# A two-layer decoder trunk on one core: moving operands read from two alternating places, and merged products in the down projections

## The chip, the core and the metric

The kernel runs on one NeuronCore of a Trainium2 chip. The metric is device time in microseconds of one execution, from the first to the last instruction with what lies around them. Three runs of the kernel before gave 567.93, 568.34 and 568.43 us.

## What is computed

One sequence of 256 tokens with 1024 features passes two layers. Layer 0 mixes tokens with a gated recurrence (RG-LRU), layer 1 with native sparse attention in three branches. Each mixer is followed by a squared-ReLU MLP with 4096 hidden features. Everything is float32. Cut to what matters:

```python
def _sq_relu_mlp(h, w_up, w_down):
    u = jax.nn.relu(h @ w_up)
    return (u * u) @ w_down

def reference(x, ...):
    for i in range(2):
        h = _rmsnorm(x, norm_mix[i])
        x = x + (_rglru_mixer(h, ...) if i == 0 else _nsa_mixer(h, ...))
        h = _rmsnorm(x, norm_ffn[i])
        x = x + _sq_relu_mlp(h, mlp_w_up[i], mlp_w_down[i])
    return _rmsnorm(x, norm_final)
```

Nearly all the arithmetic is in matrix products: the input and output projections of both mixers and, above all, the four products of the two MLPs.

## The kernel before

**Layout.** Activations lie transposed: features on the 128 partitions, the 256 tokens in the free dimension. A product takes a 128 x 128 block of weights as the stationary operand and 256 tokens of activations as the moving one, and adds into a PSUM bank of 512 columns, of which the first 256 are used (`zcols`, line 328).

**The split product.** The fast matmul type (`F32R`) keeps fewer bits than float32. So each weight piece and each activation is split in a high part, rounded to that type, and a low part, the rest. `mm3` (line 317) makes three matmuls of each 128 x 128 block: high weights with high activations, high weights with low ones, low weights with high ones. The piece of low with low is left out. The gates of the recurrence (line 686) and some small products of the attention use full float32 instead.

**Stages.** Layer 0: eight convolution chunks, gates, scan, eight branch chunks (`conv`, `gate`, `scan`, `branch`, `product`, lines 644 to 731), then the output projection. `mlp` (line 766): 32 up chunks of 8 blocks each, whose result is squared and split by `up_post` (line 776) into the tile `uhl`, high half in columns 0 to 255, low half in 256 to 511; then eight down chunks of 32 blocks each, added to the residual stream `xt` by `residual` (line 521). Layer 1: projections, compression, value projection (`values`, line 998, where the weights are the moving operand and are 304 or 256 columns wide), scores, softmax, output projection, then `mlp` again. In the last down chunk of layer 1 the residual is put into PSUM by the matmuls themselves (`seeded`, line 799).

**Weights.** 172 pieces arrive by DMA from one queue in a fixed order. ScalarE or VectorE rounds a piece to its high part (`split_hi`, line 271), VectorE subtracts for the low one (`split_lo`, line 281). In the MLPs `tick` does one such step per piece, up to six pieces ahead.

**The order.** In the MLPs the program's text sets the order of each engine. In the two mixers a planner (`Plan`, line 80) orders tasks by costs and due times that are written beside them; it sees a task's keys and cost, not its access patterns. Each engine then runs its instructions in that order.

**What the change touches.** The operands of `mm3` in `proj` (line 389), `conv`, `out` (line 758), `mlp` and `out_t` (line 1194); the moving weights of `values`; and the instructions that write those operands or read the products: lines 662, 723, 730, 731, 778, 784, 785, 887, 899, 936, 1190 and 1192. Two of them, as they stand before:

```python
dve.scalar_tensor_tensor(t, z, 0.0, rs, op0=OP.max, op1=OP.mult)      # 778
act.activation(uh[m], t, AF.Square)                                   # 784
```

Of the kernel before, what the change touches and what calls it, by code (L numbers as in the profile page):

```python
# [19 lines left out]
P = 128  # L20
# [199 lines left out]
def trunk_kernel(ctx: ExitStack, tc: tile.TileContext, x_in, vec_in, const_in, w2_in, wts, out):  # L220
# [71 lines left out]
    def later(fn):  # L292
        deferred.append(fn)
# [39 lines left out]
    class Section:  # L333
# [141 lines left out]
    hh, hl = hhl[:, :, 0], hhl[:, :, 1]  # L475
    acc = spool.tile([P, S], F32, name="acc")
# [48 lines left out]
    with ExitStack() as ph:  # L525
# [101 lines left out]
        xb, r_t, i_t, y_t, t_t, xbh, xbl = ([x[:, m] for m in range(8)] for x in (xb_b, r_b, i_b, y_b, t_b, xbh_b, xbl_b))  # L627
# [16 lines left out]
        def conv(m, t):  # L644
            b = nextbank()
            if m < NFINE:
                wh, wl, _ = sec.weight("in", 8 + m, t)
                z, zk = sec.bank(("in", 8 + m), b, zcols), ("ps", b)
                for k in range(KC):
                    def run(e, k=k):  # L650
                        w = slice(k * P, (k + 1) * P)
                        mm3(z(), wh[:, w], wl[:, w], hh[:, k], hl[:, k], k == 0, k == KC - 1)
# [9 lines left out]
            add("dve", 0.34, lambda e: e.tensor_tensor(x[:, 3:], z(), rs, op=OP.mult), r=[zk, "rs"], w=[xk], t=t)  # L662
# [58 lines left out]
        def branch(m, t):  # L721
            z, zk = sec.proj("in", m, nextbank(), t, PJ)
            add("dve", 0.34, lambda e: e.tensor_tensor(y_t[m], z(), rs, op=OP.mult), r=[zk, "rs"], w=[("y", m)], t=t + 2.6)

        def product(m, t):
            yk, hk, lk = keys("y", m), keys("xbh", m), keys("xbl", m)
            y, h, l_, x = (pair(z, m) for z in (y_b, xbh_b, xbl_b, t_b))
            add("act", 0.53, lambda e: e.activation(y, y, AF.Gelu_apprx_tanh), r=["tab"], w=yk, t=t)
            add("dve", 0.6, lambda e: e.tensor_tensor(y, y, x, op=OP.mult), r=keys("t", m), w=yk, t=t)
            add(HI2, copy(h, y), r=yk, w=hk, t=t)  # L730
            add("dve", 0.6, diff(l_, y, h), r=yk + hk, w=lk, t=t)
# [34 lines left out]
    def mlp(layer, epilogue, first, last=None):  # L766
        with ExitStack() as ph:
# [29 lines left out]
            for m in range(8):  # L797
                z = next(zrot)[:, :S]
# [612 lines left out]
```

## Time and profile before

| what | value |
|---|---|
| median of three runs (lowest, highest) | 568.34 us (567.93, 568.43) |
| span of the profiled execution | 566.4 us, so 1.9 us of the median lie around it |
| mean granted TensorE clock | 0.997 |
| TensorE busy | 559.3 us, 99% |
| VectorE busy | 407.6 us, 72% |
| ScalarE busy | 343.9 us, 61% |
| moved by DMA | 103.66 MB, 183 GB/s |

The profiled execution's whole time is not listed apart from its span, so sums are made against the span of 566.4 us and the 1.9 us are added. Busy time of TensorE counts matmuls whose ends are modelled; its pace is read from the distance between starts. A mean over the span hides that stages differ, so the rows below are taken by stretch where that matters.

### The profile page before, as it was taken

To read this page: it belongs to the slowest core of one execution; us is meant where nothing else is said; L and a number is where in the kernel's file an instruction comes from. 1 tells how busy PE (TensorE), PEld (TensorE's weight loads), DVE (VectorE), ACT (ScalarE), POOL (GpSimd) and SP (SyncE) were. 2 spreads that over 40 slices of the span, in tenths; PEclk is the share of its full clock that TensorE was granted. 3 is DMA by queue.
4 is the path that set the end of the run, shared out by engine and by line. 5 is a ranking of instruction groups with operands and counts; after the bars stand their busy time and mean duration, and the time that the engine had idled before them with its cause. 6 is when DMAs were issued, how large, how long until landed. Compare 5 with 4: busy or idle time off the path is not lost.

```text
span 566.4 us, 12406 instructions
## 1 busy us (share of the span) xinstructions
PE 559.3 (99%) x4902; PEld 552.9 (98%) x4902; DVE 407.6 (72%) x873; ACT 343.9 (61%) x670; POOL 40.1 (7%) x55
## 2 busy tenths in 40 slices
PE   9999999999999999999999999999999999999995
PEld 9989999999999999999999999999999999999995
DVE  6899989776676565466839999999767775563532
ACT  7699675866564443354647999875855664443421
POOL 1000000000000121131000000000000000222310
PEclk9999999999999999999999999999999999999998
DMA  8936467566667456555765431264766667566402
GB/s 319 407 91 220 117 219 247 176 204 192 188 192 249 155 189 217 190 181 175 276 188 166 140 99 57 75 224 138 221 200 192 196 200 233 154 202 221 132 1 74
DMA packets 33225, 103.66 MB, mean 183 GB/s; under 512 B 3856, under 2 KB 8080, under 8 KB 33168
## 3 DMA queue, kind: packets, MB, share of 16 engines
q1 hardware_dynamic: 32624, 102.42, 56.1%
q8 instruction: 38, 0.62, 0.5%
q10 hardware_dynamic: 544, 0.46, 0.2%
q14 instruction: 19, 0.16, 0.1%
HBM read 99.23 MB, written 1.05 MB: 177 GB/s over the span
## 4 chain that ended last, share of the span: by engine, by line
PE 99%; DVE 0%; ACT 0%; DVEq 0%; POOL 0%; issue 0%; POOLq 0%
PE bank L318 28%; PE bank L319 28%; PE bank L320 28%; PE bank L1177 3%; PE bank L686 2%; PE bank L1159 2%; PE bank L1105 1%; PE bank L1106 1%; PE bank L567 1%; PE bank L1012 1%; PE bank L1013 1%; PE bank L1014 1%; PE bank L953 1%; DVE xg L1295 0%; PE bank L1287 0%; DVEq L1406 0%
## 5 line engine op out<-in xcount | busy, mean ns | idle before, releaser
L318 PE MATMUL bank<-hhl,whi 128*128 128x256 f32 x768 | 213.1, 278 | 0.0
L319 PE MATMUL bank<-hhl,whi 128*128 128x256 f32 x768 | 212.4, 277 | 0.0
L320 PE MATMUL bank<-hhl,wlo 128*128 128x256 f32 x768 | 212.3, 276 | 0.0
L318 PEld LDWEIGHTS bank<-hhl,whi 128*128 128x128 f32 x768 | 144.5, 188 | 0.1
L287 DVE TENSOR_TENSOR wlo<-raw,whi 128x1024 fp32r<-128x1024 f32 x115 | 143.2, 1266 | 1.9 <-ACT whi L278 1.9
L319 PEld LDWEIGHTS bank<-hhl,whi 128*128 128x128 f32 x768 | 144.5, 188 | 0.1
L320 PEld LDWEIGHTS bank<-hhl,wlo 128*128 128x128 f32 x768 | 144.4, 188 | 0.0
L319 PE MATMUL bank<-uhl,whi 128*128 128x256 f32 x512 | 141.4, 276 | 0.0
L320 PE MATMUL bank<-uhl,wlo 128*128 128x256 f32 x512 | 141.3, 276 | 0.0
L318 PE MATMUL bank<-uhl,whi 128*128 128x256 f32 x512 | 141.3, 276 | 0.0
L278 ACT CAST whi<-raw 128x1024 fp32r<-128x1024 f32 x116 | 118.1, 1039 | 23.1 <-issue 18.8
L318 PEld LDWEIGHTS bank<-uhl,whi 128*128 128x128 f32 x512 | 96.1, 188 | 0.0
L320 PEld LDWEIGHTS bank<-uhl,wlo 128*128 128x128 f32 x512 | 96.1, 188 | 0.0
L319 PEld LDWEIGHTS bank<-uhl,whi 128*128 128x128 f32 x512 | 96.1, 188 | 0.0
L323 DVE TENSOR_TENSOR wlo<-raw,whi 128x1024 fp32r<-128x1024 f32 (+2 forms) x72 | 77.1, 1089 | 2.9 <-ACT whi L326 2.8
L326 ACT CAST whi<-raw 128x1024 fp32r<-128x1024 f32 (+2 forms) x64 | 61.2, 969 | 16.8 <-PE bank L319 7.8
L522 DVE TENSOR_TENSOR xt<-xt,bank 128x256 f32<-128x256 f32 x39 | 15.9, 417 | 74.8 <-PE bank L320 74.5
L783 ACT ACTIVATE u<-t 128x256 f32<-128x256 f32 x64 | 26.7, 418 | 58.6 <-DVE t L778 57.2
L778 DVE SCALAR_TENSOR_TENSOR t<-bank,rstd 128x256 f32<-128x256 f32 x64 | 26.9, 423 | 41.0 <-PE bank L320 40.7
L1119 ACT ACTIVATE pt<-pt,mx 128x128 f32<-128x128 f32 (+1 forms) x64 | 28.6, 450 | 1.8 <-DVE mx L1116 1.4
L785 DVE TENSOR_TENSOR uhl<-u,uhl 128x256 fp32r<-128x256 f32 x64 | 26.6, 416 | 3.0 <-ACT uhl L784 3.0
L498 ACT ACTIVATE hhl<-xt,vec 128x256 fp32r<-128x256 f32 x8 | 4.1, 510 | 39.4 <-DVE xt L522 39.4
(202 smaller groups left out, 732.6 us busy)
## 6 DMA issues: line engine op xcount, KB each, us to landing
raw<-in_dram SPq DMA_DIRECT2D x171, 512.0 KB, 4.4
raw<-in_dram SPq DMA_DIRECT2D x4, 560.0 KB, 4.6
gw<-in_dram SPq DMA_DIRECT2D x4, 512.0 KB, 8.9
raw<-in_dram SPq DMA_DIRECT2D x6, 256.0 KB, 4.9
y<-in_dram SPq DMA_DIRECT2D x2, 512.0 KB, 7.4
pT<-in_dram SPq DMA_DIRECT2D x2, 512.0 KB, 5.4
xt<-in_dram SPq DMA_DIRECT2D x3, 256.0 KB, 4.9
kl<-tl SPq DMA_DIRECT2D x8, 64.0 KB, 4.0
```

Of the source, the lines that this page charges most:

```text
L278: (act.copy if eng is None else eng.tensor_copy)(hi_t[i % NSPL][:, :n], raw_of(i)[:, :n])
L287: (eng or dve).tensor_tensor(lo[:, :n], raw_of(i)[:, :n], hi[:, :n].bitcast(F32), op=OP.subtract)
L318: pe.matmul(ps, wh, xh, start=start, stop=False)
L319: pe.matmul(ps, wh, xl, start=False, stop=False)
L320: pe.matmul(ps, wl, xh, start=False, stop=stop)
L323: return lambda e: e.tensor_tensor(o, a, h.bitcast(F32), op=OP.subtract)
L326: return lambda e: (e.copy if e is act else e.tensor_copy)(o, a)
L778: dve.scalar_tensor_tensor(t, z, 0.0, rs, op0=OP.max, op1=OP.mult)
L783: act.activation(u, t, AF.Square)
L785: later(lambda: dve.tensor_tensor(ul[m], u, uh[m].bitcast(F32), op=OP.subtract))
L1119: add("act", (0.39, 0.49)[qc], lambda e, row=row, j=j: e.activation(row, row, AF.Exp, bias=mx[:, j:j + 1], scale=-1.0, accum_out=sm[:, j:j ...
L1177: two = lambda c, w, y, **k: [e.matmul(o()[own_(hf), c0 + c.start:c0 + c.stop], w(hf), y(hf), **k) for hf in range(2)]
```

## The change

Each moving operand of the split product, formerly read in a row, is read as element 0, 128, 1, 129, ... of 256: two places, in turn. `walk` gives that view. Results land in PSUM in a row (`pairs` only gives the same 256 columns the shape 128 x 2). For tiles that hold their tokens in a row, such as `hhl`, the product's columns are then in the alternating order, and the instruction that reads them from PSUM writes its output through `walk`, which puts the tokens in order again. Tiles that are made for a product alone, `uhl`, `xbh`, `xbl`, `oh` and `ol`, are written through `walk` instead, so that the alternating reading gives tokens in order. The moving weights of `values` are put in the matching order on the host.

In the down projections `mm2` takes the place of `mm3` but in the last chunk of layer 1. One matmul with 512 moving columns takes the high weights with high and low activations side by side, into both halves of the PSUM bank; a second with 256 columns adds the low weights' product to the second half. Both halves are then added to `xt`, by two instructions.

```diff
+    def pairs(x):
+        return x.rearrange("p (a i) -> p a i", i=2)
+
+    def walk(x):
+        return x.rearrange("p (i a) -> p a i", i=2)
+
+    def walks(x):
+        return x.rearrange("p k (i a) -> p k a i", i=2)
+
     def mm3(ps, wh, wl, xh, xl, start, stop):
+        ps = pairs(ps)
         pe.matmul(ps, wh, xh, start=start, stop=False)
         pe.matmul(ps, wh, xl, start=False, stop=False)
         pe.matmul(ps, wl, xh, start=False, stop=stop)
+
+    def mm2(ps, wh, wl, xhl, xh, start, stop):
+        pe.matmul(ps.rearrange("p (h a i) -> p h a i", h=2, i=2), wh, xhl.rearrange("p (h i a) -> p h a i", h=2, i=2),
+                  start=start, stop=False)
+        pe.matmul(pairs(ps[:, S:]), wl, xh, start=False, stop=stop)
...
-            xs, xk = xs or [(hh[:, k], hl[:, k]) for k in range(KC)], xk or hkey
+            xs, xk = xs or [(hhw[:, k], hlw[:, k]) for k in range(KC)], xk or hkey
...
+    hhw, hlw = walks(hh), walks(hl)
...
-            add("dve", 0.34, lambda e: e.tensor_tensor(y_t[m], z(), rs, op=OP.mult), r=[zk, "rs"], w=[("y", m)], t=t + 2.6)
+            add("dve", 0.34, lambda e: e.tensor_tensor(walk(y_t[m]), pairs(z()), walk(rs), op=OP.mult), r=[zk, "rs"], w=[("y", m)], t=t + 2.6)
...
-            uh, ul = [x[:, :S] for x in uhl], [x[:, S:] for x in uhl]
+            uh, ul = [walk(x[:, :S]) for x in uhl], [walk(x[:, S:]) for x in uhl]
...
-                dve.scalar_tensor_tensor(t, z, 0.0, rs, op0=OP.max, op1=OP.mult)
+                dve.scalar_tensor_tensor(walk(t), pairs(z), 0.0, walk(rs), op0=OP.max, op1=OP.mult)
...
-                act.activation(uh[m], t, AF.Square)
-                later(lambda: dve.tensor_tensor(ul[m], u, uh[m].bitcast(F32), op=OP.subtract))
+                act.activation(uh[m], pairs(t), AF.Square)
+                later(lambda: dve.tensor_tensor(ul[m], pairs(u), uh[m].bitcast(F32), op=OP.subtract))
...
-                        mm3(z, wh[:, w], wl[:, w], hh[:, k], hl[:, k], k == 0, k == KC - 1)
+                        mm3(z, wh[:, w], wl[:, w], hhw[:, k], hlw[:, k], k == 0, k == KC - 1)
...
-                z = next(zrot)[:, :S]
+                zf = next(zrot)
+                z, zb = zf[:, :S], zf[:, S:]
...
-                        mm3(z, wh[:, w], wl[:, w], uh[i], ul[i], i == 0 and not seeded, i == NF - 1)
+                        if seeded:
+                            mm3(z, wh[:, w], wl[:, w], uh[i], ul[i], False, i == NF - 1)
+                        else:
+                            mm2(zf, wh[:, w], wl[:, w], uhl[i], uh[i], i == 0, i == NF - 1)
...
                         residual(z, m)
+                        residual(zb, m)
...
-                                e.matmul(ps, hh[:, k, ts_], wh[:, ws], start=(k == 0), stop=False)
+                                e.matmul(ps, hh[:, k, ts_], walk(wh[:, ws]), start=(k == 0), stop=False)
...
-    wv = np.concatenate([kv(3), win[:, D + 6 * S:], kv(5)], axis=1).reshape(KC, P, NVCOL)
+    halved = lambda w: w.reshape(D, -1, 2).transpose(0, 2, 1).reshape(D, -1)
+    wv = np.concatenate([kv(3), win[:, D + 6 * S:]], axis=1), kv(5)
+    wv = np.concatenate([halved(w) for w in wv], axis=1).reshape(KC, P, NVCOL)
```

The lines left out do the same to the other operands and results named above. The planner's costs and due times are unchanged.

The order of the instructions stays what it was, but for the merge. TensorE at the end of the last down chunk of layer 0, before (uhl the activations, whi and wlo the high and low weights):

```order
L318 MATMUL bank_3107<-uhl,whi_86 128x256
L319 MATMUL bank_3107<-uhl,whi_86 128x256
L320 MATMUL bank_3107<-uhl,wlo_93 128x256
L318 MATMUL bank_3107<-uhl,whi_86 128x256
L319 MATMUL bank_3107<-uhl,whi_86 128x256
L320 MATMUL bank_3107<-uhl,wlo_93 128x256
L318 MATMUL bank_3269<-hhl,whi_87 128x256
L319 MATMUL bank_3269<-hhl,whi_87 128x256
L320 MATMUL bank_3269<-hhl,wlo_94 128x256
```

And in the changed kernel, where L333 and L335 are the two matmuls of `mm2`:

```order
L333 MATMUL bank_2890<-uhl,whi_86 128x512
L335 MATMUL bank_2890<-uhl,wlo_93 128x256
L333 MATMUL bank_2890<-uhl,whi_86 128x512
L335 MATMUL bank_2890<-uhl,wlo_93 128x256
L333 MATMUL bank_2890<-uhl,whi_86 128x512
L335 MATMUL bank_2890<-uhl,wlo_93 128x256
L328 MATMUL bank_3021<-hhl,whi_87 128x256
L329 MATMUL bank_3021<-hhl,whi_87 128x256
L330 MATMUL bank_3021<-hhl,wlo_94 128x256
```

Two matmuls of 256 columns with the high weights have become one of 512, and TensorE has 4054 rows of this kind where it had 4534, 480 fewer.

VectorE at the same place, from the last weight split ahead of the residual on, before:

```order
L287 TENSOR_TENSOR wlo_90<-raw_82,whi_83 128x1024
L522 TENSOR_TENSOR xt<-xt,bank_3107 128x256
L501 SCALAR_TENSOR_TENSOR hhl<-xt,vec,hhl 128x256
L487 TENSOR_TENSOR sq_112<-xt 128x256
L287 TENSOR_TENSOR wlo_91<-raw_78,whi_84 128x1024
L1214 TENSOR_TENSOR acc<-acc,sq_112 128x256
```

And in the changed kernel, where the residual is line 538:

```order
L287 TENSOR_TENSOR wlo_90<-raw_82,whi_83 128x1024
L538 TENSOR_TENSOR xt<-xt,bank_2890 128x256 x2
L517 SCALAR_TENSOR_TENSOR hhl<-xt,vec,hhl 128x256
L503 TENSOR_TENSOR sq_112<-xt 128x256
L287 TENSOR_TENSOR wlo_91<-raw_78,whi_84 128x1024
L1239 TENSOR_TENSOR acc<-acc,sq_112 128x256
```

The residual is there twice, ahead of the low half of the next input; all else on VectorE stands where it stood.

## Rows read from the trace of the kernel before

**Rows 1.** The page's first lines and its first part: the span, and of each engine the busy time, its share of the span and its instructions.
```profile
span 566.4 us, 12406 instructions
...
PE 559.3 (99%) x4902; PEld 552.9 (98%) x4902; DVE 407.6 (72%) x873; ACT 343.9 (61%) x670; POOL 40.1 (7%) x55
```

**Rows 2.** The view of waits, of TensorE alone: the waiting line, whom it waited for; us in total, times, the longest.
```profile
PE bank L567 <- POOL warm L562: 1.3, 1, 1.3
PE bank L1281 <- ACT sqh L1278: 0.3, 1, 0.3
```

**Rows 3.** The chain of work that ended last: its shares of the span by line, and pieces of it in order of time (start us, us, what, how many instructions of one kind in a row). L686 is the gates' product, L953 the compression's hidden layer, L1159 the transposes of the attention weights.
```profile
by line: PE bank L318 28.3%; PE bank L319 28.3%; PE bank L320 28.3%; PE bank L1177 2.6%; PE bank L686 2.4%; PE bank L1159 1.9%; PE bank L1105 1.1%; PE bank L1106 1.1%; PE bank L567 0.9%; PE bank L1012 0.8%; PE bank L1013 0.7%; PE bank L1014
...
29.64 12.95 PE bank L686 x60
...
284.14 3.62 PE bank L953 x64
...
312.87 0.65 PE bank L1159 x6
```

**Rows 4.** Groups of instructions by line and shape, of TensorE (PE) and of its weight loads (PEld): line, engine, operation, out<-in, tile, shape, count, then busy us and mean ns of one, then idle time before them. Lines 319 and 320 have the same counts as line 318.
```profile
L318 PE MATMUL bank<-hhl,whi 128*128 128x256 f32 x768 | 213.1, 278 | 0.0
...
L318 PEld LDWEIGHTS bank<-hhl,whi 128*128 128x128 f32 x768 | 144.5, 188 | 0.1
...
L318 PE MATMUL bank<-uhl,whi 128*128 128x256 f32 x512 | 141.3, 276 | 0.0
...
L318 PE MATMUL bank<-oh,whi 128*128 128x256 f32 x64 | 18.1, 283 | 0.0
...
L318 PE MATMUL bank<-xbh,whi 128*128 128x256 f32 x64 | 17.7, 276 | 0.0
...
L686 PE MATMUL bank<-xb,gw 128*128 128x256 f32 x64 | 14.1, 379 | 0.0
L1159 PE MATMUL bank<-cst,pt 128*128 128x128 f32 x96 | 13.3, 274 | 0.0
...
L1159 PEld LDWEIGHTS bank<-cst,pt 128*128 128x128 f32 x96 | 10.7, 141 | 0.5 <-issue 0.5
...
L953 PEld LDWEIGHTS bank<-pt,pT 128*64 128x64 f32 x64 | 3.5, 152 | 0.1
```

**Rows 5.** TensorE in order of time, in the down projection of layer 0: start us, us, engine, line, operation. The ends of matmuls are modelled; the pace is read from the starts. 20 rows of the same kind are left out.
```profile
199.73 0.28 PE L319 MATMUL bank<-uhl,whi 128*128 128x256 f32 x1
199.84 0.28 PE L320 MATMUL bank<-uhl,wlo 128*128 128x256 f32 x1
199.96 0.28 PE L318 MATMUL bank<-uhl,whi 128*128 128x256 f32 x1
200.07 0.28 PE L319 MATMUL bank<-uhl,whi 128*128 128x256 f32 x1
...
202.45 0.28 PE L319 MATMUL bank<-uhl,whi 128*128 128x256 f32 x1
```

**Rows 6.** Busy time by stretch: the stretch, its us, then busy us and instructions of PE, PEld, DVE, ACT and POOL, the granted clock, the DMA share and GB/s. In order: start and first convolutions; gates and scan; down projection of layer 0; attention.
```profile
0.00:20.00 20.00, 18.73 (x144) 18.73 (x144) 14.88 (x34) 14.51 (x31) 1.70 (x12) 1.00 0.92 343
20.00:60.00 40.00, 40.00 (x296) 38.35 (x297) 38.92 (x80) 38.00 (x70) 2.17 (x7) 1.00 0.56 196
...
180.00:268.00 88.00, 88.00 (x779) 88.00 (x778) 48.75 (x51) 35.63 (x41) 17.80 (x19) 1.00 0.58 193
...
300.00:380.00 80.00, 80.00 (x753) 76.41 (x752) 76.85 (x365) 69.98 (x214) 0.19 (x2) 1.00 0.39 122
```

**Rows 7.** TensorE in order of time, in the value projection of the attention (columns as in rows 5): three matmuls of 304 columns, then three of 256.
```profile
291.51 0.30 PE L1012 MATMUL bank<-whi,hhl 128*128 128x304 f32 x1
291.65 0.30 PE L1013 MATMUL bank<-wlo,hhl 128*128 128x304 f32 x1
291.79 0.30 PE L1014 MATMUL bank<-whi,hhl 128*128 128x304 f32 x1
291.93 0.28 PE L1012 MATMUL bank<-whi,hhl 128*128 128x256 f32 x1
292.04 0.28 PE L1013 MATMUL bank<-wlo,hhl 128*128 128x256 f32 x1
...
292.28 0.30 PE L1012 MATMUL bank<-whi,hhl 128*128 128x304 f32 x1
```

**Rows 8.** Groups of VectorE's instructions by line and shape (columns as in rows 4): the split of weights, the first and the last step behind an up projection, the residual.
```profile
L287 DVE TENSOR_TENSOR wlo<-raw,whi 128x1024 fp32r<-128x1024 f32 x115 | 143.2, 1266 | 1.9 <-ACT whi L278 1.9
...
L778 DVE SCALAR_TENSOR_TENSOR t<-bank,rstd 128x256 f32<-128x256 f32 x64 | 26.9, 423 | 41.0 <-PE bank L320 40.7
L785 DVE TENSOR_TENSOR uhl<-u,uhl 128x256 fp32r<-128x256 f32 x64 | 26.6, 416 | 3.0 <-ACT uhl L784 3.0
L522 DVE TENSOR_TENSOR xt<-xt,bank 128x256 f32<-128x256 f32 x39 | 15.9, 417 | 74.8 <-PE bank L320 74.5
```

**Rows 9.** TensorE in order of time at the end of layer 0 (columns as in rows 5): the last matmul of the down projection and the first of the next section.
```profile
261.38 0.28 PE L320 MATMUL bank<-uhl,wlo 128*128 128x256 f32 x1
261.50 0.28 PE L318 MATMUL bank<-hhl,whi 128*128 128x256 f32 x1
```

**Rows 10.** VectorE in order of time at the same place (in brackets the idle time before and what ended it): the last residual, and the low half of the normalised chunk 7.
```profile
261.70 0.42 DVE L522 TENSOR_TENSOR xt<-xt,bank 128x256 f32<-128x256 f32 x1 [4.61 <-PE bank L320]
262.69 0.48 DVE L501 SCALAR_TENSOR_TENSOR hhl<-xt,vec,hhl 128x256 fp32r<-128x256 f32 x1 [0.58 <-ACT hhl L498]
```

More of the change, by code (lines that the diff above doesn't have):

```diff
@@ L626, in trunk_kernel @@
         xbh_b, xbl_b = (rg.tile([P, 8, S], F32R, name=n) for n in ("xbh", "xbl"))
-        xb, r_t, i_t, y_t, t_t, xbh, xbl = ([x[:, m] for m in range(8)] for x in (xb_b, r_b, i_b, y_b, t_b, xbh_b, xbl_b))
+        xbhw, xblw = walks(xbh_b), walks(xbl_b)
+        xb, r_t, i_t, y_t, t_t, xbh, xbl = ([x[:, m] for m in range(8)] for x in (xb_b, r_b, i_b, y_b, t_b, xbhw, xblw))
         pair = lambda x, m: x[:, m // 2 * 2:m // 2 * 2 + 2]
@@ L651, in run @@
                         w = slice(k * P, (k + 1) * P)
-                        mm3(z(), wh[:, w], wl[:, w], hh[:, k], hl[:, k], k == 0, k == KC - 1)
+                        mm3(z(), wh[:, w], wl[:, w], hhw[:, k], hlw[:, k], k == 0, k == KC - 1)
                         if m == 0 and k == 1:
@@ L661, in conv @@
             bk = ("xb", m)
-            add("dve", 0.34, lambda e: e.tensor_tensor(x[:, 3:], z(), rs, op=OP.mult), r=[zk, "rs"], w=[xk], t=t)
+            add("dve", 0.34, lambda e: e.tensor_tensor(walk(x[:, 3:]), pairs(z()), walk(rs), op=OP.mult), r=[zk, "rs"], w=[xk], t=t)
             add("act", 0.49, lambda e: e.activation(xb[m], x[:, 3:], AF.Identity, bias=col(V_CB, m), scale=cw(3, m)),
@@ L722, in branch @@
             z, zk = sec.proj("in", m, nextbank(), t, PJ)
-            add("dve", 0.34, lambda e: e.tensor_tensor(y_t[m], z(), rs, op=OP.mult), r=[zk, "rs"], w=[("y", m)], t=t + 2.6)
+            add("dve", 0.34, lambda e: e.tensor_tensor(walk(y_t[m]), pairs(z()), walk(rs), op=OP.mult), r=[zk, "rs"], w=[("y", m)], t=t + 2.6)
         def product(m, t):
             yk, hk, lk = keys("y", m), keys("xbh", m), keys("xbl", m)
-            y, h, l_, x = (pair(z, m) for z in (y_b, xbh_b, xbl_b, t_b))
+            y, h, l_, x = (pair(z, m) for z in (y_b, xbhw, xblw, t_b))
+            yw = y.rearrange("p k (a i) -> p k a i", i=2)
             add("act", 0.53, lambda e: e.activation(y, y, AF.Gelu_apprx_tanh), r=["tab"], w=yk, t=t)
             add("dve", 0.6, lambda e: e.tensor_tensor(y, y, x, op=OP.mult), r=keys("t", m), w=yk, t=t)
-            add(HI2, copy(h, y), r=yk, w=hk, t=t)
-            add("dve", 0.6, diff(l_, y, h), r=yk + hk, w=lk, t=t)
+            add(HI2, copy(h, yw), r=yk, w=hk, t=t)
+            add("dve", 0.6, diff(l_, yw, h), r=yk + hk, w=lk, t=t)
         at_ = {}
@@ L854, in trunk_kernel @@
         oht, olt = (at.tile([P, 8 * S], F32R, name=n) for n in ("oh", "ol"))
-        oh, ol = ([x[:, i * S:(i + 1) * S] for i in range(8)] for x in (oht, olt))
+        ohw, olw = (walks(x.rearrange("p (k s) -> p k s", s=S)) for x in (oht, olt))
+        oh, ol = ([x[:, i] for i in range(8)] for x in (ohw, olw))
         NPT_ = 16
@@ L886, in qchunk @@
             ak, bk = ("sa", c % NQ), ("sb", c % NQ)
-            add("dve", 0.4, lambda e: e.scalar_tensor_tensor(x, z(), cst[:, C_QS + c:C_QS + c + 1], rs,
+            add("dve", 0.4, lambda e: e.scalar_tensor_tensor(walk(x), pairs(z()), cst[:, C_QS + c:C_QS + c + 1], walk(rs),
                                                              op0=OP.mult, op1=OP.mult), r=[zk, "rs"], w=[xk], t=t)
@@ L898, in kchunk @@
             x, xk, l_, lk = turn()
-            add("dve", 0.34, lambda e: e.tensor_tensor(x, z(), rs, op=OP.mult), r=[zk, "rs"], w=[xk], t=t)
+            add("dve", 0.34, lambda e, x=x: e.tensor_tensor(walk(x), pairs(z()), walk(rs), op=OP.mult), r=[zk, "rs"], w=[xk], t=t)
             x, l_ = two_blocks(x), two_blocks(l_)
@@ L935, in cproj @@
             x, xk, _, _ = turn()
-            add("dve", 0.34, lambda e: e.tensor_tensor(x, z(), rs, op=OP.mult), r=[zk, "rs"], w=[xk], t=t)
+            add("dve", 0.34, lambda e, x=x: e.tensor_tensor(walk(x), pairs(z()), walk(rs), op=OP.mult), r=[zk, "rs"], w=[xk], t=t)
             for hf in range(2):
@@ L1010, in run @@
                                 ws = slice(kk * NVCOL + c0, kk * NVCOL + c0 + ncol[b])
-                                ps = vz[h][b]()
-                                e.matmul(ps, hh[:, k, ts_], wh[:, ws], start=(k == 0), stop=False)
-                                e.matmul(ps, hh[:, k, ts_], wl[:, ws], start=False, stop=False)
-                                e.matmul(ps, hl[:, k, ts_], wh[:, ws], start=False, stop=(k == KC - 1))
+                                ps = pairs(vz[h][b]())
+                                e.matmul(ps, hh[:, k, ts_], walk(wh[:, ws]), start=(k == 0), stop=False)
+                                e.matmul(ps, hh[:, k, ts_], walk(wl[:, ws]), start=False, stop=False)
+                                e.matmul(ps, hl[:, k, ts_], walk(wh[:, ws]), start=False, stop=(k == KC - 1))
                         add("pe", 0.77, run, r=wk + [hkey[k]], w=[("ps", banks[h][0]), ("ps", banks[h][1])],
@@ L1171, in pv @@
             o = zview(("o", js[0]), 7, lambda x: x[:, :n * S])
-            cols = slice(js[0] * S, (js[-1] + 1) * S)
+            oj = slice(js[0], js[-1] + 1)
+            ow = lambda: o().rearrange("p (k a i) -> p k a i", k=n, i=2)
             def run(e):
@@ L1189, in pv @@
             ok, lk = ([(x, j) for j in js] for x in ("oh", "ol"))
-            add([("act", 0.1 + 0.24 * n, 0.0), ("dve", 0.07 + 0.27 * n, 0.2)], lambda e: copy(oht[:, cols], o())(e), r=bk, w=ok,
+            add([("act", 0.1 + 0.24 * n, 0.0), ("dve", 0.07 + 0.27 * n, 0.2)], lambda e: copy(ohw[:, oj], ow())(e), r=bk, w=ok,
                 t=t + 1.9 * n)
-            add("dve", 0.07 + 0.27 * n, lambda e: diff(olt[:, cols], o(), oht[:, cols])(e), r=bk + ok, w=lk, t=t + 1.9 * n + 0.3)
+            add("dve", 0.07 + 0.27 * n, lambda e: diff(olw[:, oj], ow(), ohw[:, oj])(e), r=bk + ok, w=lk, t=t + 1.9 * n + 0.3)
         def out_t(half, m, b, t, step):
```

## The prediction, made before the changed kernel ran

> **What bounds the kernel now.** I read the page's first part, then TensorE's waits, then its rows in order of time, because a share of 99% alone does not say what sets the pace. The span is 566.4 us and TensorE is busy for 559.3 us of it [rows 1]. It waits for others only 1.6 us in all [rows 2]. So the time is nearly the sum of the steps from one matmul start to the next, and the question is what one step costs.
>
> Of that sum the split product (lines 318 to 320) has 28.3% three times, 84.9% of 566.4 = 480.9 us [rows 3]. Its 4224 instructions are three times 768 + 512 + 64 + 64 [rows 4], so a step is 113.85 ns on average. In the down projection 24 steps take 202.45 − 199.73 = 2.72 us, or 113.3 ns each [rows 5]. The granted clock there is 1.00, the 2.4 GHz level [rows 6]; 256 columns at one per tick would be 106.7 ns. Each step thus pays a surcharge of 6.7 ns, 7.2 in the mean.
>
> Whose surcharge is it? Three kinds of row tell. The full-precision matmuls of the gates make two records each for 256 columns, and 60 records take 12.95 us: 215.8 ns, which is 512 ticks (213.3 ns) plus 2.5 [rows 3]. The transposes take 0.65 us for six, 108.3 ns [rows 3]. So where a column stays two ticks, an instruction pays about 2.5 ns, however long. In the value projection three steps of 304 columns take 0.42 us (140 ns, surcharge 13.3) and three of 256 take 0.35 us (117 ns, surcharge 10) [rows 7]. There the surcharge grows with the columns. I read it as a loss in the stream of moving columns when it runs at one per tick, and not as a fixed price of an instruction.
>
> **The change, part by part.**
>
> *Alternating reads.* Every moving operand of the split product, and that of the value projection, is read as element 0, 128, 1, 129 and so on. No row has such a stream. Bounds: at best the surcharge falls to the 2.5 ns of the gates, 106.7 + 2.5 = 109.2 ns. At worst a column costs two ticks, as in the gates, 215.8 ns. The nearest row to strided reading is the compression's hidden layer, 62 columns in steps of 16 elements: 64 records in 3.62 us, two side by side, 113 ns or 1.8 ns a column, against 0.84 in the gates [rows 3]; loads of weights may be what sets it, so it excludes nothing. I take the good end. The surcharge appears only in the full-rate stream, so feeding that stream is the narrow place, and two places could take turns to deliver, one being fetched while the other is read. That part is a guess; only the place of the loss is read from rows.
>
> The SBUF Cachelines part of the Trainium skill's page "Advanced Engine Details and Errata" (section Memory Cachelines) speaks against this: reads want at least two hits in one 16-byte line, and a new line at every access is penalised. By that rule the stream slows down, which is the third rival; no row here shows an alternating stream, so the trace neither confirms nor refutes it.
>
> *The merge.* In 15 of 16 down-projection chunks, 32 pairs each, the high weights take 512 columns at once: 480 pairs become single matmuls. At best one costs 215.8 ns [rows 3], against 2 × 109.2 = 218.4; if the surcharge stays, 2 × 113.3 = 226.7 at most. I take 215.8. It also removes 480 weight loads of 128 columns; each lies beside a matmul now [rows 4].
>
> *The sum.* Left are 4224 − 960 = 3264 steps of 256 columns and 480 of 512: 3264 × 109.2 = 356.4, 480 × 215.8 = 103.6, together 460.0 instead of 480.9: −20.9 us, of which the merge has 480 × 2.6 ns = 1.2. The value projection has 48 matmuls of each width: 48 × 140 + 48 × 117 = 12.3 us [rows 7] becomes 48 × 129.2 + 48 × 109.2 = 11.4: −0.9. Together −21.8.
>
> The isolated-gap formula of the page "TensorE: Matmul & The Clock Gate" of the Trainium skill (section Back-to-back issue gap), N/2.4 + 2.5 ns warm, gives 109.2 ns for a contiguous 256-column matmul, so by it nothing would be left to save. The trace disagrees: 113.3 ns in the loop.
>
> *What is given back.* From 20 to 60 us VectorE is busy 38.9 of 40, from 300 to 380 us 76.9 of 80 [rows 6]; a faster TensorE must wait for it there. About 230 and 312 of the steps (296 in the first window less 64 gates; nine projections of 24 and eight of 12 in the second) save 4.65 ns each: 1.1 + 1.5 us, which I count as lost. In the first 20 us the DMA share is 0.92 [rows 6]: another 120 × 4.65 = 0.6. Net −21.8 + 3.2 = −18.6.
>
> *The other engines.* 160 VectorE instructions of 256 elements and 8 of 512 now write, or read and write, alternating places, and so do 64 and 7 on ScalarE. No row has that pattern. Below, it costs nothing. Above, I double the cost per element: (1266 − 416)/768 = 1.1 ns [rows 8], so 0.28 us per instruction. In the up projections a chunk needs 1266 + 423 + 416 = 2.1 us of VectorE [rows 8] against 24 × 109.2 = 2.62 of TensorE, so up to 0.52 more is hidden. I take nothing: VectorE asks for an element every 1.1 ns, and TensorE gets one every 0.44 ns (113.3/256) from the same memory, so VectorE has more slack for a jump. The doubled price is the first rival.
>
> *The second residual.* Fifteen more instructions of 417 ns [rows 8]; VectorE has 39 us free in the down projection's 88 [rows 6]. Where the next reader is near, at the end of layer 0, the last residual starts at 261.70 and the low half of chunk 7 is done at 262.69 + 0.48 = 263.18 [rows 9, 10]. TensorE starts on the next projections at 261.50, and by its order 42 matmuls of other chunks come first: 42 × 113.3 ns = 4.8 us, so chunk 7 is wanted at 266.3. The slack of 3.1 us covers 0.42. Nothing is queued behind that residual but splits, two to five pieces ahead. In layer 1 the last chunk keeps the old form, so the end is unchanged. No DMA is added or moved.
>
> Between the profiled span and the median of the runs (568.34) lie 1.9 us, which stay. Result: 568.3 − 18.6 = 549.7 us.
>
> **The rivals.**
>
> *One: strided writes double VectorE's price.* The up projections then need 2.1 + 0.57 = 2.67 us a chunk against 2.62: 58 chunks × 0.05 = 3 us. The two tight windows pay directly: at most 16 × 0.28 = 4.5 us, and 9 × 0.28 + 4 × 0.57 = 4.8. Time 549.7 + 12.3 = 562. For it: both windows are full. Against it: VectorE is far from full elsewhere.
>
> *Two: the surcharge belongs to the weight load.* Every matmul carries its own load [rows 4], and 6.7 ns could be the hand-over. Alternation then gives nothing and only the 480 dropped loads count: 480 × 6.7 = 3.2 us, 565.1. For it: the steady step never varies, 0.11 or 0.12 us in every row of that stretch [rows 5]. Against it: the transposes carry a load each and step at 108.3, and the surcharge of 304 columns exceeds that of 256.
>
> *Three, slower: the alternating stream stalls.* Each column lies 128 elements from the one before; at two ticks a column a step costs 215.8 ns, a merged one 2 × 213.3 + 2.5 = 429.1. 3264 × 215.8 + 480 × 429.1 = 910 us instead of 481: about 998. It decides as soon as 256 alternating columns cost more than 113.9 ns. For it: the one strided row pays 1.8 ns a column. Against it: that row carries two weight loads for 62 columns.
>
> **How the numbers follow.** Forecast 0.52 (545 to 554). Rival one 0.16 (555 to 564). Rival two 0.11 (565). Rival three 0.12. Rival one without any gain on TensorE 0.03: 565 + 12 = 577, slower. No effect beyond 0.2%, which is about what a measurement of this kernel can tell: 0.06. Faster is 0.52 + 0.16 + 0.11 = 0.79, same 0.06, slower 0.12 + 0.03 = 0.15. The range of 543 to 566 holds the first three, 0.79; its lower end allows a give-back of nothing and a step down to 108.
>
> **What would show it.** Right: steps of 109 ns in the up projections, 216 and 109 alternating in the down projections, about 480 fewer TensorE instructions, and waits of TensorE on VectorE at 20 to 60 and 300 to 380 us only. Rival one: lines 778 and 785's successors well over 423 and 416 ns. Rival two: 113 ns steps in the up projections. Rival three: steps far over 114 ns there. The forecast is wrong if the step in the up projections is not within 108 to 111 ns.

## The result, and the profile after

The changed kernel takes 562.8 us in the median (562.43 to 563.95) against 568.25 for the kernel before, four runs of each: a ratio of 0.9907, 95% interval 0.9893 to 0.9921. It is faster, as forecast, but by 5.4 us and not by 18.6. The profile is that of the slowest of the four runs, 563.95 us. The page's first lines answer to [rows 1]:

```profile
span 561.8 us, 11456 instructions
...
PE 550.5 (98%) x4422; PEld 528.5 (94%) x4422; DVE 436.3 (78%) x888; ACT 358.0 (64%) x670; POOL 40.1 (7%) x55
```

The span fell by 4.6 us. TensorE is still busy for 98% of it, yet its weight loads went from 98% to 94% and VectorE from 72% to 78%. Two views say what a step costs now. First TensorE in order of time in the up projections of layer 0 (start us, us, engine, line, operation), the loop in which nothing is merged:

```profile
149.80 0.28 PE L330 MATMUL bank<-hhl,wlo 128*128 128x256 f32 x1
149.91 0.28 PE L328 MATMUL bank<-hhl,whi 128*128 128x256 f32 x1
...
151.92 0.28 PE L328 MATMUL bank<-hhl,whi 128*128 128x256 f32 x1
```

From 149.80 to 151.92 there are 19 steps, 111.6 ns each. Before it was 113.3 in the down projection [rows 5]. The same view in the down projection:

```profile
199.93 0.38 PE L333 MATMUL bank<-uhl,whi 128*128 128x512 f32 x1
200.15 0.27 PE L335 MATMUL bank<-uhl,wlo 128*128 128x256 f32 x1
200.26 0.38 PE L333 MATMUL bank<-uhl,whi 128*128 128x512 f32 x1
...
201.90 0.38 PE L333 MATMUL bank<-uhl,whi 128*128 128x512 f32 x1
```

From 199.93 to 201.90 there are six blocks, 328 ns each. Before, a block was three steps of 113.3, 340 ns. The rows' starts alternate by 0.22 and 0.11: over all 480 pairs the mean from start to start is 218.3 ns from a wide matmul to the next narrow one and 109.2 from a narrow one to the next wide one.

The work behind an up projection became dearer. The groups by line and shape, of all engines, answer to [rows 4] and [rows 8] (count, then busy us and mean ns of one, then idle time before). The first two are the weight loads of the down projection, one of 128 columns for each wide and each narrow matmul, as before:

```profile
L335 PEld LDWEIGHTS bank<-uhl,wlo 128*128 128x128 f32 x480 | 92.2, 192 | 0.0
L333 PEld LDWEIGHTS bank<-uhl,whi 128*128 128x128 f32 x480 | 90.7, 189 | 12.6
...
L802 ACT ACTIVATE uhl<-t 128x256 fp32r<-128x256 f32 x64 | 42.5, 664 | 0.0
L803 DVE TENSOR_TENSOR uhl<-u,uhl 128x256 fp32r<-128x256 f32 x64 | 40.8, 638 | 2.7 <-ACT uhl L802 2.6
L796 DVE SCALAR_TENSOR_TENSOR t<-bank,rstd 128x256 f32<-128x256 f32 x64 | 39.5, 622 | 22.7 <-PE bank L330 22.6
```

The same view of VectorE alone, for the branch results of layer 0 and the low half of its output projection's operand, which are written alternating too:

```profile
L740 DVE TENSOR_TENSOR y<-bank,rstd 128x256 f32<-128x256 f32 x8 | 4.9, 618 | 0.0
...
L338 DVE TENSOR_TENSOR xbl<-y,xbh 128x512 fp32r<-128x512 f32 x4 | 4.4, 1099 | 0.1
```

Three of them before, in the same views (ScalarE's square, the branch result, the low half):

```profile
L784 ACT ACTIVATE uhl<-t 128x256 fp32r<-128x256 f32 x64 | 25.8, 403 | 0.0
L723 DVE TENSOR_TENSOR y<-bank,rstd 128x256 f32<-128x256 f32 x8 | 3.3, 410 | 0.0
L323 DVE TENSOR_TENSOR xbl<-y,xbh 128x512 fp32r<-128x512 f32 x4 | 2.7, 673 | 0.0
```

The instructions of 256 elements went from 423 to 622 ns (line 778, now 796) and from 416 to 638 (785, now 803), both [rows 8]; the ScalarE square (784, now 802) takes 664 ns where line 784's mean was 403 before. So alternating access adds 0.20 to 0.26 us. The branch result rose from 410 to 618, the 512-element step from 673 to 1099. The square only writes alternating; VectorE's instructions also read an operand that way, so what a write alone costs there isn't told apart.

Whether that is felt depends on the stretch. Busy time by stretch (us; then PE, PEld, DVE, ACT, POOL with their counts; clock, DMA share, GB/s):

```profile
60.00:74.00 14.00, 12.28 (x104) 11.56 (x103) 14.00 (x20) 7.93 (x10) 0.00 (x0) 1.00 0.46 146
95.00:180.00 85.00, 85.00 (x751) 84.64 (x750) 71.96 (x101) 60.36 (x99) 0.00 (x0) 1.00 0.62 203
180.00:268.00 88.00, 88.00 (x565) 81.62 (x564) 55.29 (x62) 37.20 (x43) 17.77 (x19) 1.00 0.60 202
```

And the kernel before in the first of them:

```profile
60.00:74.00 14.00, 14.00 (x126) 14.00 (x125) 14.00 (x21) 7.94 (x11) 0.00 (x0) 1.00 0.60 174
```

From 60 to 74 us, where the branch results and their split pieces are made, VectorE was full before and is full now; TensorE lost 1.7 of its 14 us. In the up projections VectorE is busy 72 of 85 us and hides its dearer steps. The weight loads are busy for 84.6 of 85 us there; that doesn't make them the limit, for they were busy all the time before, too (88.00 of 88 in the down projections, [rows 6]).

TensorE's waits answer to [rows 2] (line, releaser; us in total, times, longest):

```profile
PE bank L583 <- POOL warm L578: 1.3, 1, 1.3
PE bank L329 <- DVE xbl L338: 1.2, 2, 1.0
PE bank L329 <- DVE ol L338: 0.7, 1, 0.7
PE bank L328 <- ACT xbh L341: 0.5, 1, 0.5
PE bank L1036 <- DVE tt L960: 0.4, 1, 0.4
PE bank L328 <- DVE tt L960: 0.4, 1, 0.4
...
```

The first was there before. The others are new: xbh, xbl and ol are operands of the output projections that are written alternating, and tt takes results of the projections of layer 1. The chain of waits between 61.5 and 70 us (start us, us, what) runs through VectorE alone:

```profile
62.06 0.47 DVE y L740
62.52 0.94 DVE xbl L338
63.46 1.05 DVE wlo L338
64.52 0.59 DVE y L747
...
```

No link of it is TensorE: branch results (L740), their products (L747), the low halves (xbl) and the split of weights follow each other without a gap, and the output projection waits for them. Before, the chain from 62 to 70 us held nothing but steps of the split product:

```profile
by line: PE bank L319 34.5%; PE bank L320 34.1%; PE bank L318 32.8%
```

By landmarks in TensorE's rows (first and last matmul that reads a given tile), the 4.6 us divide as in the table. It also has the single profiles of five of the experiments below. Entries are differences to the kernel before in us; negative is faster.

| stretch (us before) | change | E2 | E3 | E4 | E5 | E6 |
|---|---|---|---|---|---|---|
| start to the first xbh (65.1) | −0.1 | −0.8 | −0.3 | −0.1 | −0.9 | −0.7 |
| output projection, layer 0 (22.5) | +2.5 | +2.5 | +0.2 | −0.1 | +1.4 | +1.1 |
| up projections, layer 0 (86.8) | −1.4 | −1.4 | 0.0 | −1.4 | −1.4 | −1.4 |
| down projections, layer 0 (87.1) | −3.3 | −1.4 | +2.3 | −3.3 | −3.3 | −3.3 |
| mixer of layer 1 (122.0) | +1.9 | +0.2 | +1.0 | +0.2 | +1.2 | −0.7 |
| up projections, layer 1 (87.4) | −1.3 | −1.3 | 0.0 | −1.3 | −1.3 | −1.3 |
| down projections, layer 1 (87.2) | −3.0 | −1.3 | +2.2 | −3.0 | −3.0 | −3.0 |

The MLPs gained 9.0 us; the mixers gave 4.3 back. What is left behind the last row, 8.4 us, is the same in all. The start and the mixer of layer 1 differ by up to 1.7 us between kernels that do the same there (the change and E2), so only the other rows are read closely.

A DMA has a part in that spread. In the mixer of layer 1 VectorE's L960, which writes tt, also waits until a DMA has read what tt held (count, busy us, mean ns, idle us and what ended it):

```profile
L960 DVE TENSOR_TENSOR tt<-bank,rstd 128x256 f32<-128x256 f32 x4 | 2.3, 604 | 1.5 <-DMA pt<-tt 1.4
```

That wait is 0.3 us before, 1.4 in the change, 0.8 in E4, 1.8 in E5, and there is none in E2 and E6. TensorE's waits for tt are 0.8 us in the change and 1.5 in E5, but 0.2 to 0.4 in E2, E4 and E6. So the 1.9 us of the change in this row can't be put down to alternating writes alone: E2 has the same instructions there and 0.2.

### The profile page after: what moved, and what is told of

It reads as the page before. It is cut to its first block, busy times and chain, and to the rows that moved or that the text cites. A ratio compares the mean times of both kernels' runs of the same rounds, so it can differ in the third digit from the quotient of the medians.

```text
span 561.8 us, 11456 instructions
## 1 busy us (share of the span) xinstructions
PE 550.5 (98%) x4422; PEld 528.5 (94%) x4422; DVE 436.3 (78%) x888; ACT 358.0 (64%) x670; POOL 40.1 (7%) x55
## 4 chain that ended last, share of the span: by engine, by line
PE 73%; DVE 18%; DMA 5%; ACT 2%; issue 1%; SPq 0%; POOL 0%; DVEq 0%; ACTq 0%; POOLq 0%
PE bank L333 19%; PE bank L329 13%; PE bank L330 13%; PE bank L328 13%; PE bank L335 9%; DVE wlo L338 4%; DMA raw<-in_dram 3%; DVE pt L1140 2%; DMA gw<-in_dram 2%; DVE pt L1168 2%; DVE xb L683 1%; DMA pt<-tt 1%; DVE tt L911 1%; DVE t L735 1%; PE bank L1036 1%
## 5 line engine op out<-in xcount | busy, mean ns | idle before, releaser
L333 PE MATMUL bank<-uhl,whi 128*128 128x512 f32 x480 | 157.3, 382 | 0.0
L328 PEld LDWEIGHTS bank<-hhl,whi 128*128 128x128 f32 x768 | 147.7, 192 | 0.6 <-DVE tt L960 0.4
L329 PEld LDWEIGHTS bank<-hhl,whi 128*128 128x128 f32 x768 | 147.7, 192 | 0.0
L335 PE MATMUL bank<-uhl,wlo 128*128 128x256 f32 x480 | 130.8, 273 | 0.0
L333 PEld LDWEIGHTS bank<-uhl,whi 128*128 128x128 f32 x480 | 90.7, 189 | 12.6
L335 PEld LDWEIGHTS bank<-uhl,wlo 128*128 128x128 f32 x480 | 92.2, 192 | 0.0
L538 DVE TENSOR_TENSOR xt<-xt,bank 128x256 f32<-128x256 f32 x54 | 22.3, 419 | 62.2 <-PE bank L335 60.2
L796 DVE SCALAR_TENSOR_TENSOR t<-bank,rstd 128x256 f32<-128x256 f32 x64 | 39.5, 622 | 22.7 <-PE bank L330 22.6
L803 DVE TENSOR_TENSOR uhl<-u,uhl 128x256 fp32r<-128x256 f32 x64 | 40.8, 638 | 2.7 <-ACT uhl L802 2.6
L802 ACT ACTIVATE uhl<-t 128x256 fp32r<-128x256 f32 x64 | 42.5, 664 | 0.0
L1295 ACT ACTIVATE xg<-xt,vec 128x256 f32<-128x256 f32 x7 | 3.6, 508 | 37.7 <-DVE xt L538 37.7
```

What stands on the lines that cost most here:

```text
L333: pe.matmul(ps.rearrange("p (h a i) -> p h a i", h=2, i=2), wh, xhl.rearrange("p (h i a) -> p h a i", h=2, i=2), start=start, stop=False)
L335: pe.matmul(pairs(ps[:, S:]), wl, xh, start=False, stop=stop)
L796: dve.scalar_tensor_tensor(walk(t), pairs(z), 0.0, walk(rs), op0=OP.max, op1=OP.mult)
L802: act.activation(uh[m], pairs(t), AF.Square)
L803: later(lambda: dve.tensor_tensor(ul[m], pairs(u), uh[m].bitcast(F32), op=OP.subtract))
```

## The experiments

**Theory L**: read from two places, the stream costs one tick per column and the 2.5 ns; what holds an unmerged step at 111.6 ns is the load of its 128 weight columns. **Rival S**: the alternating stream still loses a share of its columns. **Theory G**: the give-back is the price of alternating writes on VectorE and ScalarE where those are full. Its rivals are named in each run. The ratios stand beside runs of the kernel before of the same session: 568.13 us for E2 to E4, 567.95 for E5 and E6.

### E1: the stream by itself

Twelve stretches of 60 matmuls on constant data, ahead of the kernel's own work, while no other engine uses the data. The weights (`warm`) are zeros, the moving operand (`big`) ones; `two(n)` reads n elements of it from two alternating places. Four of them, each with its line's number:

```diff
+        for _ in N:
+            pe.matmul(wf[:, :256], warm[:, :P], big[:, :256], start=True, stop=True)                     # 579
+        for _ in N:
+            pe.matmul(as2(wf[:, :256]), warm[:, :P], two(256), start=True, stop=True)                    # 581
+        for _ in N:
+            pe.matmul(wf[:64, :256], warm[:, :64], big[:, :256], start=True, stop=True)                  # 583
+        for _ in N:
+            pe.matmul(as2(wf[:64, :256]), warm[:, :64], two(256), start=True, stop=True)                 # 585
```

> The kernel before, with twelve stretches of 60 matmuls of the fast type put ahead of its work; the time in all means nothing, the steps in the stretches do. Theory L (the alternating stream itself is free, and the load of 128 weight columns sets a floor of 111.4 ns): 256 columns in a row 113.3 ns; alternating 111.4 with 128 weight columns and 109.2 with 64; 320 columns in a row 141.7, alternating 135.8; 512 in a row 226.7, alternating 215.8. Rival S (the alternating stream still loses in proportion to its columns, 4.4%): alternating 256 is 111.4 with 64 weight columns too, 320 is 139.2, 512 is 222.8. If the loss in a row belonged to the weight load, 256 in a row with 64 weight columns would fall to 109.2 as well. Places 4 or 16 elements apart, every second element, and four places are there to see what makes the difference; by L any of them that leaves the stream free steps at 111.4.

The chain of waits, its pieces in order of time (start us, us, line, count):

```profile
10.47 6.82 PE bank L579 x60
17.29 6.70 PE bank L581 x60
23.98 7.14 PE bank L583 x60
31.13 6.55 PE bank L585 x60
37.68 8.80 PE bank L587 x60
46.48 8.15 PE bank L589 x60
54.63 14.00 PE bank L591 x60
68.63 12.95 PE bank L593 x60
...
94.98 13.80 PE bank L599 x60
108.78 8.59 PE bank L601 x60
117.37 2.16 PE bank L568 x18
```

Each piece divided by its count is a step. The last piece belongs to the kernel's own warm-up behind the stretches: 256 columns in a row with 128 weight columns, weights and moving operand from one tile.

| line | moving operand | weight columns | ns |
|---|---|---|---|
| 579 | 256 in a row | 128 | 113.7 |
| 581 | 256 alternating | 128 | 111.7 |
| 583 | 256 in a row | 64 | 119.0 |
| 585 | 256 alternating | 64 | 109.2 |
| 587, 589 | 320 in a row, alternating | 128 | 146.7, 135.8 |
| 591, 593 | 512 in a row, alternating | 128 | 233.3, 215.8 |
| 595, 597 | 256, places 4 and 16 elements apart | 128 | 111.7, 111.7 |
| 599 | 256, every second element of 512 | 128 | 230.0 |
| 601 | 256, four places in turn | 128 | 143.2 |
| 568 | 256 in a row, from the tile of the weights | 128 | 120.0 |

Theory L's numbers for alternating streams come out within 0.3 ns. Alternating, 256, 320 and 512 columns cost 106.7, 133.3 and 213.3 ns of ticks plus 2.5, if the weight load is short or the stream long; only 256 columns with 128 weight columns stand at 111.7. S is refuted three times. For streams in a row the expectation fails: 146.7 ns where it had 141.7, and 233.3 where it had 226.7. There the stream costs 9 to 12% more than its ticks, and the 113.7 ns of the kernel's own shape is the best case of it, not the rule. Half the load did not make that step shorter (119.0): the load had not set it. Nor does a full load alone bring it down to 113, for line 568 has one and takes 120.0. Why the kernel's loops settle at 113 the runs don't show.

The load that holds the alternating step at 111.7 is not a floor under every step. In the merged loop of the change the load for the next wide matmul, of 128 columns too, starts with the narrow matmul (both at 200.15 us), and the step is 109.2 all the same. So line 585 need not owe its 109.2 to its 64 rows of output, for the narrow matmul writes 128. The 2.4 ns are there where every 256 columns have a load of 128 columns, and gone where the load is half as wide. In the merged loop the narrow step lacks them, but the wide one takes 218.3 ns where line 593 has 215.8. Whether the load's price has moved there, and how a load holds a step at all, isn't shown.

What helps is two places, and not their distance: 4 elements do as well as 128. Four places in turn take 36.5 ns over their ticks, a step of two elements doubles the time.

### E2: alternating reads without the merge

```diff
-                        if seeded:
-                            mm3(z, wh[:, w], wl[:, w], uh[i], ul[i], False, i == NF - 1)
-                        else:
-                            mm2(zf, wh[:, w], wl[:, w], uhl[i], uh[i], i == 0, i == NF - 1)
+                        mm3(z, wh[:, w], wl[:, w], uh[i], ul[i], i == 0 and not seeded, i == NF - 1)
...
-                        residual(zb, m)
```

> The changed kernel without the merge: three matmuls a block in the down projections, alternating reads everywhere. Theory L: steps of 111.4 ns there, 334 ns a block instead of 327.5, 480 blocks, so 562.8 + 3.2 = 566.0 us. Rival (only the dropped weight loads carry the gain): no faster than before, 568.2 us or more, with 113.3 ns steps in the down projections.

Measured: 564.96 us, ratio 0.9944 (0.993 to 0.9957). The steps in the down projection are 111.3 to 112.0 ns in the mean. Theory L's number is missed by 1 us, and the table has 1.7 us less than the change in the mixer of layer 1, where the two do the same; the two down stretches have −2.7 us where the change has −6.3, so the merge is worth 3.6 us there, against 3.2 expected. Alternation alone gains, and the merge adds to it.

### E3: the merge without alternating reads

```diff
+    def mm2(ps, wh, wl, xhl, xh, start, stop):
+        pe.matmul(ps, wh, xhl, start=start, stop=False)
+        pe.matmul(ps[:, S:], wl, xh, start=False, stop=stop)
...
-                        mm3(z, wh[:, w], wl[:, w], uh[i], ul[i], i == 0 and not seeded, i == NF - 1)
+                        if seeded:
+                            mm3(z, wh[:, w], wl[:, w], uh[i], ul[i], False, i == NF - 1)
+                        else:
+                            mm2(zf, wh[:, w], wl[:, w], uhl[i], uh[i], i == 0, i == NF - 1)
```

> The kernel before with the merge alone, all reads in a row. Theory L with a loss of the stream in proportion to its columns: 512 columns cost 226.7 ns and a block 340 ns as before, 568.2 us, no change. Rival (the surcharge of 6.7 ns is a fixed price of a weight load): a block costs 333.3 ns, 480 x 6.7 = 3.2 us less, 565.0 us.

Measured: 574.12 us, ratio 1.0105 (1.0091 to 1.0119): slower, which neither had. TensorE in order of time in the down projection of layer 0:

```profile
199.72 0.39 PE L323 MATMUL bank<-uhl,whi 128*128 128x512 f32 x1
199.95 0.28 PE L324 MATMUL bank<-uhl,wlo 128*128 128x256 f32 x1
200.07 0.39 PE L323 MATMUL bank<-uhl,whi 128*128 128x512 f32 x1
...
201.11 0.39 PE L323 MATMUL bank<-uhl,whi 128*128 128x512 f32 x1
```

From 199.72 to 201.11 there are four blocks, 348 ns each, against 340 before. The means are 230.8 ns behind the wide matmul and 118.8 behind the narrow one: 480 × 9.6 ns = 4.6 us, and the two stretches lost 4.5. E1 has nearly the same two numbers for streams in a row, 233.3 and 119.0. My expectation took 113.3 ns for the stream's own price; it is the price of one loop, and the merge left that loop: even the narrow matmul, whose shape and load stayed, went from 113.3 to 118.8. So the merge pays only with alternating reads.

### E4: alternating reads where they cost nothing

All projections of both mixers and both their output projections go back to reading and writing in a row; the MLPs and the value projection keep the change.

```diff
-            xs, xk = xs or [(hhw[:, k], hlw[:, k]) for k in range(KC)], xk or hkey
+            xs, xk = xs or [(hh[:, k], hl[:, k]) for k in range(KC)], xk or hkey
...
-        xbhw, xblw = walks(xbh_b), walks(xbl_b)
+        xbhw, xblw = xbh_b, xbl_b
...
-        ohw, olw = (walks(x.rearrange("p (k s) -> p k s", s=S)) for x in (oht, olt))
+        ohw, olw = (x.rearrange("p (k s) -> p k s", s=S) for x in (oht, olt))
```

> The changed kernel with alternating reads kept in both MLPs (merge included) and in the value projection, and taken back in all other projections and in both output projections of the mixers. Theory G (the gain was given back by strided writes of VectorE and ScalarE on the way of the mixers): the MLPs keep their 9.0 us, the values give 0.8, the mixers cost what they did before: 568.2 - 9.8 = 558.4 us. Rival (a faster TensorE only runs into VectorE's work, which was near full anyway): the give-back stays, 562 us or more.

Measured: 559.53 us, ratio 0.9847 (0.9833 to 0.986), the fastest kernel here, 1.1 us short of theory G's number. The MLPs keep their 9.0 us and the mixers lose nothing that can be told. The 0.8 us of the value projection don't show: its steps are 129 and 111 ns as in the change, but the mixer around it has +0.2. Its waits of TensorE, complete:

```profile
PE bank L584 <- POOL warm L579: 1.3, 1, 1.3
PE bank L1307 <- ACT sqh L1304: 0.2, 1, 0.2
PE bank L328 <- DVE tt L961: 0.2, 1, 0.2
```

And its busy time from 60 to 74 us, VectorE full as before, but TensorE too:

```profile
60.00:74.00 14.00, 14.00 (x125) 14.00 (x124) 14.00 (x22) 7.74 (x11) 0.00 (x0) 1.00 0.60 183
```

Nothing new waits but the 0.2 us for tt, and VectorE's full stretch is no obstacle as long as its instructions stay what they were. The rival is not settled by this run alone, because it slows TensorE in the mixers down again as well. Against it speaks the sign: a TensorE that only runs into unchanged work loses its gain, but does not end the output projection of layer 0 later than before, as the change does by 2.4 us (−0.1 and +2.5 in the table). E6, below, leaves TensorE its alternating reads.

### E5 and E6: reads or writes

E5 takes back only the output projections' operands, in both writing and reading:

```diff
-        xbhw, xblw = walks(xbh_b), walks(xbl_b)
+        xbhw, xblw = xbh_b, xbl_b
...
-            yw = y.rearrange("p k (a i) -> p k a i", i=2)
+            yw = y
...
-        ohw, olw = (walks(x.rearrange("p (k s) -> p k s", s=S)) for x in (oht, olt))
+        ohw, olw = (x.rearrange("p (k s) -> p k s", s=S) for x in (oht, olt))
...
-            ow = lambda: o().rearrange("p (k a i) -> p k a i", k=n, i=2)
+            ow = lambda: o().rearrange("p (k s) -> p k s", k=n)
```

> The changed kernel with one part taken back: the operands of both mixers' output projections are written and read in a row; all else alternates. Theory G (strided writes of those operands make TensorE wait): the output projection of layer 0 gets back 2.5 us and that of layer 1 about 1.0, so 562.8 - 3.5 = 559.3 us, and the waits on xbl, xbh and ol are gone. Rival (the waits come from the whole chain of strided steps before, the projections' results above all): the waits stay in good part, 561 us or more.

E6 writes them in a row and reads them alternating:

```diff
-            y, h, l_, x = (pair(z, m) for z in (y_b, xbhw, xblw, t_b))
-            yw = y.rearrange("p k (a i) -> p k a i", i=2)
+            y, h, l_, x = (pair(z, m) for z in (y_b, xbh_b, xbl_b, t_b))
+            yw = y
...
-            add("dve", 0.07 + 0.27 * n, lambda e: diff(olw[:, oj], ow(), ohw[:, oj])(e), r=bk + ok, w=lk, t=t + 1.9 * n + 0.3)
+            add("dve", 0.07 + 0.27 * n, lambda e: diff(olt.rearrange("p (k s) -> p k s", s=S)[:, oj], ow(), oht.rearrange("p (k s) -> p k s", s=S)[:, oj])(e), r=bk + ok, w=lk, t=t + 1.9 * n + 0.3)
```

> The changed kernel with the operands of both mixers' output projections written in a row but still read from two alternating places; the tokens of those two products come out in another order, so that part of the result is changed, and the amount of work is not. Theory G (the strided writes are to blame, not the alternating reads): the waits go as in the run before and the steps of those projections stay at 111.4 ns, 384 x 2 ns less than with reads in a row, so about 558.5 us. Rival (the alternating reads of these operands are to blame): the time stays near 562.8 us.

Measured: E5 560.48 us, ratio 0.9866 (0.9851 to 0.988); E6 559.74 us, ratio 0.9854 (0.9838 to 0.9871). E6 refutes its rival: with alternating reads of these operands left in place, 3.1 us come back, so the reads are not what delayed. Both miss theory G's number by 1.2 us. Waits of TensorE that are left, of E5 and then of E6:

```profile
PE bank L1036 <- DVE tt L960: 1.1, 1, 1.1
PE bank L329 <- DVE xbl L338: 0.9, 1, 0.9
```

```profile
PE bank L329 <- DVE xbl L338: 0.9, 1, 0.9
PE bank L328 <- DVE tt L960: 0.4, 1, 0.4
```

The waits on xbh and ol are gone, a part of the wait on xbl (0.9 of 1.2 us) stays, although xbl itself is nearly as cheap as before (0.69 us). So I put too much on the operands: of the 2.5 us in layer 0's output projection 1.1 and 1.4 came back. The rest fits the steps ahead of them, the convolution and branch results, which E4 also makes cheap again and which cost 8 × 0.2 us each; no run takes them back by themselves, so that part is argued and not shown. There E5's rival was half right. The wait on tt in E5 lies behind the DMA named under the table; E6, with the same writes there, has no such wait of VectorE.

## Why the prediction was wrong

**What held.** The sign, the place of the loss, and that two alternating places cure it. The surcharge was in the stream of moving columns: E1 has 109.2 ns for 256 columns with 64 weight columns, 215.8 for 512, and the value projection in the changed kernel 129 ns for 304, where it was 140. Why two places help stays the guess that it was. The third rival is refuted. With it goes, for TensorE's reads, the rule about two hits in a 16-byte line that the Trainium skill states in "Advanced Engine Details and Errata" (Memory Cachelines): two places in turn touch another line at every column and are the fastest, while every second element, two hits a line, takes twice the time. Nor is another line at every column enough, for four places in turn touch one too and take 143.2 ns. For VectorE and ScalarE the rule points the right way: alternating places cost them 0.20 to 0.26 us an instruction. The formula N/2.4 + 2.5 of the Trainium skill's page "TensorE: Matmul & The Clock Gate" (Back-to-back issue gap) agrees with the alternating streams of E1 at 320 and 512 columns, and at 256 with 64 weight columns; with 128 weight columns 256 take 111.7 instead of its 109.2.

**What failed: the step of 109.2 ns.** It was mis-sized: the steps measured 111.6, which is outside the 108 to 111 that the prediction itself set as its sign. I took the 2.5 ns from the gates and the transposes [rows 3] and let the transposes, with a load each, exclude a floor from the load. But their load is another one: 141 ns in the mean, against 188 [rows 4]. The fast type's load beside 256 columns was never seen without a slower stream in front of it, so a second limit close behind the first could not be read from the trace, and should have been an end of the range. 2784 unmerged steps × 2.4 ns = 6.7 us. Merged blocks cost 218.3 + 109.2 = 327.5 ns instead of 325.0: 480 × 2.5 = 1.2 us more. Their narrow step is the forecast's; the wide one was mis-sized, and why isn't shown (E1 has 215.8).

**What failed: strided writes at no price.** The forecast took nothing from a range of 0 to 0.28 us; measured are 0.20 to 0.26. The argument from how seldom VectorE asks for an element was no argument: the same layout that TensorE read faster was written more slowly by VectorE and ScalarE. Rival one had the price about right and its place wrong. That its 562 us is nearly the 562.8 measured is luck: it has TensorE save all that the forecast has, and 12.3 us paid on top. Rival one looked at 20 to 60 and 300 to 380 us and at the up projections; the up projections hid it all. It hurt from 60 to 74 us, a stretch that I did not list though VectorE was at 14.00 of 14 there. The mixers lost 4.3 us; by a step of 111.6 alone they would have gained about 3 (2 × 576 steps × 1.8 ns, as the up projections gained, and 0.8 in the values). That is a give-back of 7, where the forecast had 3.2. Of it only the 2.5 us of layer 0's output projection are tied to alternating places by experiments (all of it by E4, 1.1 to 1.4 by E5 and E6); E2, with the same mixers, lost 1.9 in them and not 4.3.

**The rest** is in the mean step of 113.85 ns. It held 0.5 ns of waits and slow first steps, which a faster stream does not remove: 4224 × 0.5 = 2.1 us. In the trace before, 19 of these steps take over 130 ns, and together they hold 2.0 us beyond 113.3 ns a step. The parts add up to 6.7 + 1.2 + 4 + 2.1 = 14.0, which is the gap between the forecast and the measured fall of the span, 18.6 − 4.6. For the mixers the sum closes by construction, since the 4 is what their measured loss leaves beyond the other terms; in the MLPs it is a check.

**Rival two** had the right part in the wrong role: the load was not the limit before (119.0 ns with half of it), and after the change its width decides between 111.7 and 109.2 (E1).

**The second residual**: VectorE had room in the down projections (55.3 of 88 us busy), and no wait of TensorE in the changed kernel is on hhl, which the residual leads to; a smaller cost can't be told from the spread of the stretch behind it.

## What to carry to other kernels

When a limit is lifted, the gain runs only to the next one; measure the next one by itself, in the same type and shape, ahead of the sum. A new operand layout is paid for by whoever writes it, so alternate only where the writer has time: E4 keeps the MLPs, drops the mixers, and is 1.5% faster than the start where the full change is 0.9%. A merge should be tried together with what makes it pay, and by itself: here it lost 1.1% alone.

## What was not expected of the hardware

- A stream of the fast type in a row costs 9 to 12% over its ticks in three stretches of E1 (119.0 ns for 256 columns, 146.7 for 320, 233.3 for 512), but 113.3 to 113.7 for 256 columns in the kernel's loop and in E1's copy of it. A full load of 128 weight columns goes with both: E1's line 568 takes 120.0, and the narrow step of E3 118.8.
- Two places in turn, 4 to 128 elements apart, remove that; four in turn (143.2 ns) or one place with a step of two (230.0) do not.
- Where each matmul of 256 alternating columns has its own load of 128 weight columns of that type, the step is 111.6 to 111.7 ns; with 64 weight columns it is 109.2, and so is the narrow step of the merged loop beside a load of 128, where the wide step takes 218.3 and not the 215.8 of E1.
- Alternating places cost VectorE (reading and writing) 0.20 to 0.22 us and ScalarE (writing) 0.26 us per 256 elements, about 0.8 and 1.0 ns an element.
